# Query-key scores: casting loads of four heads replaced by float32 loads of eight heads that GpSimd casts and interleaves

## The chip, the cores and the metric

The kernel runs on one core of one Trainium2 chip. The metric is the device time of the kernel in microseconds (us), as the median of several runs. Engine names are those of the profile: PE is TensorE, PEld its weight loads, DVE is VectorE, ACT is ScalarE, POOL is GpSimd, SP is SyncE. "L106" is line 106 of the kernel that was profiled.

## The reference

```python
# q and k: (8, 12, 1024, 64) float32, normal random numbers times 0.1
def reference(q, k):
    return np.einsum('bhid,bhjd->bhij', q, k).astype(np.float32)
```

There are 96 heads. Each needs a 1024x1024 float32 score matrix from two 1024x64 inputs. The kernel reads 50.33 MB and must write 402.65 MB, so it is mostly a kernel that writes.

## The kernel before

Heads are taken in batches of four (the first three batches have 1, 1 and 2 heads). The loads are issued by GpSimd, and they cast: they read float32 from memory and leave float16 in the core's own memory. PE transposes q in pairs of 64 columns, and k twice, so that every transposed k row exists in both halves of the 128 rows. Score matmuls then alternate between the two halves. DVE copies the transposes out of PSUM, ACT and DVE copy the scores, and SP issues one 4 MB output transfer a head.

```python
    in_pool = ctx.enter_context(tc.tile_pool(name="in_pool", bufs=4))
    out_pool = ctx.enter_context(tc.tile_pool(name="out_pool", bufs=4))
    ...
        def load(self):                                   # class Batch
            rows = slice(self.first * S, (self.first + self.G) * S)
            self.q_sb = in_pool.tile([P, GMAX * NT, D], F16, tag="q")
            self.k_sb = in_pool.tile([P, GMAX * NT, D], F16, tag="k")
            for src, dst in ((qf, self.q_sb), (kf, self.k_sb)):
                nc.gpsimd.dma_start(
                    out=dst[:, : self.R],
                    in_=src[rows].rearrange("(p r) d -> p r d", p=P),
                )
        def transpose(self, a):
            ...
            for e in range(4):
                r = a * NT + 2 * e
                nc.tensor.transpose(t_ps[:, e], self.q_sb[:, r : r + 2], ident)
            for t in range(NT):
                rows = self.k_sb[:, a * NT + t]
                nc.tensor.transpose(t_ps[0:64, 4 + t], rows, ident)
                nc.tensor.transpose(t_ps[64:128, 4 + t], rows, ident)
            ...                                           # DVE: G copies to qT, one to kT
        def scores(self, g):
            o_sb = out_pool.tile([P, NT, S], F32, tag="out")
            for t in range(NT):
                h = (t % 2) * 64                          # alternating half of the rows
                ps = po_pool.tile([P, S], F32, tag="po")
                for n in range(2):
                    nc.tensor.matmul(ps[:, n * 512 : (n + 1) * 512],
                                     qT[h : h + 64, g, t // 2],
                                     kT[h : h + 64, g, n * 512 : (n + 1) * 512])
                ...                                       # t in (1, 4, 6): DVE copies, else ACT
            nc.sync.dma_start(out=..., in_=...)           # 4 MB, one head
    ...
    AHEAD = 3                                             # loads three batches ahead
```

The output pool holds four buffers of 32 KB for each partition. That is the queue of work that keeps the DMA engines busy when something else stalls.

## Time and profile before

| | before |
|---|---|
| time, median of 3 runs | 1070.94 us (1070.71 to 1071.27) |
| DMA busy share | 9 tenths or more in all 40 slices but the last |
| loading queue's share of 16 engines | 11.9% |
| output: issue to landing | 36.7 us |
| PE / DVE / ACT / POOL busy | 59 / 53 / 44 / 3% |

These are lines of the profile's page: busy time by engine, then the rows of 40 equal slices of the span (a digit is the busy share in tenths), the DMA queues, the summary of the chain of waits, three groups of instructions (busy us, mean ns of one, idle time before them and what ended most of it), and the output's DMA issues.

```profile
PE 627.9 (59%) x3456; PEld 214.0 (20%) x3456; DVE 565.7 (53%) x758; ACT 468.4 (44%) x481; POOL 28.2 (3%) x58
...
DMA  9999999999999999999999999999999999999996
GB/s 213 394 382 386 380 400 414 394 420 396 410 410 384 422 398 410 411 389 419 401 397 424 390 419 401 400 419 389 415 406 399 422 430 430 429 434 432 431 431 292
...
q1 hardware_dynamic: 13824, 402.66, 88.0%
q0 software_dynamic: 7488, 25.17, 11.9%
q8 instruction: 27, 0.44, 0.1%
...
DMA 77%; PE 7%; ACT 7%; DVE 1%; issue 0%; ACTq 0%
...
L106 PE MATMUL ps<-kT,qT 64*128 64x512 f16 x1536 | 480.9, 597 | 270.8 <-ACT o_sb L114 227.2
...
L91 DVE COPY qT<-t_ps 128x128 f16<-128x128 f16 (+1 forms) x374 | 121.2, 469 | 95.7 <-PE t_ps L82 95.7
L92 DVE COPY kT<-t_ps 128x1024 f16<-128x1024 f16 x96 | 118.8, 1237 | 0.0
...
out_dram<-o_sb SPq DMA_DIRECT2D x96, 4096.0 KB, 36.7
```

The DMA engines are the bottleneck: no other engine is above 59%, and the DMA row has no hole. (The rate reads 380 to 420 GB/s while loads run, because the casting loads count with the 25.17 MB that they write, not the 50.33 MB that they read; after the last load it is about 431.) The Trainium skill, "DMA: Bandwidth & Descriptors", section "Where 436 GB/s comes from", puts the ceiling of the fabric at 435 GB/s, and the trace agrees: the slices without loads, but for the last, reach 429 to 434.

The chain of waits (start, duration, what) shows the same thing in time. One long output transfer follows another with about 6 us of PE and ACT between them, in which the other queued outputs keep the engines busy.

```profile
793.69 38.04 DMA out_dram<-o_sb
...
835.00 1.48 PE ps L106 x4
...
837.53 34.88 DMA out_dram<-o_sb
```

Three windows of before: the columns are the window, its length, busy time of PE, PEld, DVE, ACT and POOL with counts, the granted PE clock, the DMA share and GB/s. The first is in the middle, and the other two are at the end, where the engines finish one after another.

```profile
322.00:330.00 8.00, 5.22 (x36) 2.06 (x33) 5.27 (x8) 4.17 (x5) 0.56 (x2) 0.50 1.01 400
...
1062.00:1066.00 4.00, 0.00 (x0) 0.00 (x0) 0.00 (x0) 0.00 (x0) 0.00 (x0) 0.50 0.19 82
1066.00:1070.00 4.00, 0.00 (x0) 0.00 (x0) 0.00 (x0) 0.00 (x0) 0.00 (x0) 0.50 0.02 8
```

### The profile page before, as it was taken

To read this page: it belongs to the slowest core of one execution; us is meant where nothing else is said; L and a number is where in the kernel's file an instruction comes from. 1 tells how busy PE (TensorE), PEld (TensorE's weight loads), DVE (VectorE), ACT (ScalarE), POOL (GpSimd) and SP (SyncE) were. 2 spreads that over 40 slices of the span, in tenths; PEclk is the share of its full clock that TensorE was granted. 3 is DMA by queue.
4 is the path that set the end of the run, shared out by engine and by line. 5 is a ranking of instruction groups with operands and counts; after the bars stand their busy time and mean duration, and the time that the engine had idled before them with its cause. 6 is when DMAs were issued, how large, how long until landed. Compare 5 with 4: busy or idle time off the path is not lost.

```text
span 1069.6 us, 8844 instructions
## 1 busy us (share of the span) xinstructions
PE 627.9 (59%) x3456; PEld 214.0 (20%) x3456; DVE 565.7 (53%) x758; ACT 468.4 (44%) x481; POOL 28.2 (3%) x58
## 2 busy tenths in 40 slices
PE   6786455565654656557465564655656567667530
PEld 2222121121211212212122121221211212212100
DVE  5676445464653646547455464554655646655420
ACT  4454344444533445344443444444444445454530
POOL 3000000000000000000000000000000000000000
PEclk8565555555555555555555555555555555555555
DMA  9999999999999999999999999999999999999996
GB/s 213 394 382 386 380 400 414 394 420 396 410 410 384 422 398 410 411 389 419 401 397 424 390 419 401 400 419 389 415 406 399 422 430 430 429 434 432 431 431 292
DMA packets 21353, 428.39 MB, mean 401 GB/s; under 512 B 2368, under 2 KB 2880, under 8 KB 9024
## 3 DMA queue, kind: packets, MB, share of 16 engines
q1 hardware_dynamic: 13824, 402.66, 88.0%
q0 software_dynamic: 7488, 25.17, 11.9%
q8 instruction: 27, 0.44, 0.1%
q14 instruction: 14, 0.11, 0.0%
HBM read 50.33 MB, written 402.65 MB: 424 GB/s over the span
## 4 chain that ended last, share of the span: by engine, by line
DMA 77%; PE 7%; ACT 7%; DVE 1%; issue 0%; ACTq 0%
DMA out_dram<-o_sb 77%; ACT o_sb L114 7%; PE ps L106 6%; DVE kT L92 0%; DVE qT L91 0%; PE t_ps L81 0%; PE t_ps L78 0%; DVE o_sb L112 0%; PE t_ps L82 0%; ACTq L114 0%
## 5 line engine op out<-in xcount | busy, mean ns | idle before, releaser
L114 ACT COPY o_sb<-ps 128x1024 f32<-128x1024 f32 x480 | 467.1, 1014 | 566.5 <-DMA out_dram<-o_sb 359.1
L106 PE MATMUL ps<-kT,qT 64*128 64x512 f16 x1536 | 480.9, 597 | 270.8 <-ACT o_sb L114 227.2
L112 DVE COPY o_sb<-ps 128x1024 f32<-128x1024 f32 x288 | 351.7, 1223 | 374.0 <-DMA out_dram<-o_sb 213.8
L106 PEld LDWEIGHTS <-qT 64*128 64x128 f16 x1536 | 101.0, 109 | 605.2 <-issue 580.0
L91 DVE COPY qT<-t_ps 128x128 f16<-128x128 f16 (+1 forms) x374 | 121.2, 469 | 95.7 <-PE t_ps L82 95.7
L78 PE MATMUL t_ps<-ident,q_sb 128*128 128x128 f16 x384 | 56.4, 299 | 135.9 <-DVE kT L92 130.2
L92 DVE COPY kT<-t_ps 128x1024 f16<-128x1024 f16 x96 | 118.8, 1237 | 0.0
L81 PE MATMUL t_ps<-ident,k_sb 128*64 128x128 f16 x768 | 102.5, 310 | 0.0
L82 PE MATMUL t_ps<-ident,k_sb 128*64 128x128 f16 x768 | 102.4, 310 | 0.0
L81 PEld LDWEIGHTS <-k_sb 128*64 128x64 f16 x768 | 77.5, 165 | 19.8 <-issue 19.4
L82 PEld LDWEIGHTS <-k_sb 128*64 128x64 f16 x768 | 77.4, 164 | 7.5 <-issue 7.5
L78 PEld LDWEIGHTS <-q_sb 128*128 128x128 f16 x384 | 34.6, 127 | 187.2 <-issue 121.3
L64 POOL DMA_DIRECT2D q_sb<-in_q_dram x26 | 14.0, 537 | 767.5 <-PE t_ps L78 766.8
L64 POOL DMA_DIRECT2D k_sb<-in_k_dram x26 | 13.9, 534 | 13.2 <-PE t_ps L82 13.2
L114 ACT ACT_TABLE_LOAD x1 | 1.3, 1283 | 0.7 <-PEq L157 0.7
masks.py:199 POOL TENSOR_SCALAR_AFFINE_SELECT ident<-ident 128x128 f16<-128x128 f16 x1 | 0.4, 362 | 0.0
masks.py:197 POOL MEMSET ident<- 128x128 f16 x1 | 0.3, 271 | 0.0
L157 POOL MEMSET const-float32-0.0<- 128x1 f32 x1 | 0.1, 98 | 0.2 <-issue 0.2
L157 POOL MEMSET const-bfloat16-1.0<- 128x1 bf16 x1 | 0.1, 101 | 0.0
L157 POOL MEMSET const-uint8-127<- 128x1 uint8 x1 | 0.1, 101 | 0.0
L157 POOL MEMSET const-float32-1.0<- 128x1 f32 x1 | 0.1, 98 | 0.0
## 6 DMA issues: line engine op xcount, KB each, us to landing
out_dram<-o_sb SPq DMA_DIRECT2D x96, 4096.0 KB, 36.7
q_sb<-in_q_dram POOLq DMA_DIRECT2D x23, 512.0 KB, 18.1
k_sb<-in_k_dram POOLq DMA_DIRECT2D x23, 512.0 KB, 29.4
q_sb<-in_q_dram POOLq DMA_DIRECT2D x2, 128.0 KB, 3.5
k_sb<-in_k_dram POOLq DMA_DIRECT2D x2, 128.0 KB, 3.6
q_sb<-in_q_dram POOLq DMA_DIRECT2D x1, 256.0 KB, 6.3
k_sb<-in_k_dram POOLq DMA_DIRECT2D x1, 256.0 KB, 7.0
```

The costliest lines, as they stand in the source:

```text
L64: nc.gpsimd.dma_start(out=dst[:, : self.R], in_=src[rows].rearrange("(p r) d -> p r d", p=P),)
L78: nc.tensor.transpose(t_ps[:, e], self.q_sb[:, r : r + 2], ident)
L81: nc.tensor.transpose(t_ps[0:64, 4 + t], rows, ident)
L82: nc.tensor.transpose(t_ps[64:128, 4 + t], rows, ident)
L91: nc.vector.tensor_copy(out=qT[:, g, :, :, a], in_=t_ps[:, 0:4, ms])
L92: nc.vector.tensor_copy(out=kT[:, :, :, a], in_=t_ps[:, 4:12].rearrange("c t (g m) -> c g m t", g=G),)
L106: nc.tensor.matmul(ps[:, n * 512 : (n + 1) * 512], qT[h : h + 64, g, t // 2], kT[h : h + 64, g, n * 512 : (n + 1) * 512],)
L112: nc.vector.tensor_copy(out=o_sb[:, t], in_=ps)
L114: nc.scalar.copy(out=o_sb[:, t], in_=ps)
L157: nc = _bacc.Bacc("TRN2", target_bir_lowering=False, num_devices=1)
```

## The change

The intent: plain float32 loads instead of casting ones, issued by ACT and SP instead of GpSimd; the idle GpSimd does the cast. Heads come in blocks of eight, in two halves of four. The cast writes head a of the first half beside head a of the second half, so that one 128x128 transpose serves two heads and k need not be transposed twice. A block has four loads of 8 KB a partition (q and k of each half), but only three raw buffers fit, so the fourth load of a block waits for the first cast of that block. There is only one float16 block buffer.

```diff
-    in_pool = ctx.enter_context(tc.tile_pool(name="in_pool", bufs=4))
+    in_pool = ctx.enter_context(tc.tile_pool(name="in_pool", bufs=3))
+    half_pool = ctx.enter_context(tc.tile_pool(name="half_pool", bufs=1))
 ...
+        def load(self, n, eng, raw=None):
+            if raw is None:
+                x_sb = in_pool.tile([P, self.elems], F32, tag="x")
+                raw = x_sb
+            self.raw[n] = raw
+            start = (self.first + n // 2 * self.G) * S
+            src = (qf, kf)[n % 2][start : start + self.G * S]
+            eng.dma_start(out=raw, in_=src.rearrange("(p r) d -> p (r d)", p=P))
 ...
+        def cast(self, n):
+            nc.gpsimd.tensor_copy(
+                out=self.halves[n % 2][:, :, n // 2],
+                in_=self.raw[n].rearrange("p (r d) -> p r d", d=D),
+            )
 ...
-            for e in range(4):
-                r = a * NT + 2 * e
-                nc.tensor.transpose(t_ps[:, e], self.q_sb[:, r : r + 2], ident)
-            for t in range(NT):
-                rows = self.k_sb[:, a * NT + t]
-                nc.tensor.transpose(t_ps[0:64, 4 + t], rows, ident)
-                nc.tensor.transpose(t_ps[64:128, 4 + t], rows, ident)
+            for x, src in enumerate(self.halves):
+                for t in range(NT):
+                    nc.tensor.transpose(t_ps[:, x * NT + t], src[:, a * NT + t], ident)
 ...                                  (DVE: one copy of 128x1024 to qT, one to kT)
-                h = (t % 2) * 64
+            cs = slice(half * D, (half + 1) * D)          (all matmuls of a head in one half)
 ...
+    def refill(i):                                        (i: the block after the next)
+        if b:
+            half_sb = half_pool.tile([P, 2 * half_elems], F16, tag="half")
+            b.place(half_sb, 0)
+            for n in range(3):
+                b.cast(n)
+        yield                                             (one head later)
+        if b:
+            b.load(3, nc.scalar)
+            b.cast(3)
+        if c:                                             (c: the block after b)
+            c.load(0, nc.scalar)
+            c.load(1, nc.scalar)
+        yield
+        yield
+        if c:
+            c.load(2, nc.scalar)
```

The first eight heads are loaded in smaller pieces into a borrowed output buffer.

More of the change, by code (lines that the diff above doesn't have):

```diff
@@ L28 @@
     GMAX = 4
-    assert D == 64 and NT == 8 and BH % GMAX == 0
+    assert D == 64 and NT == 8 and BH % (2 * GMAX) == 0
     qf = q.rearrange("b h s d -> (b h s) d")
@@ L37 @@
     of = out.rearrange("b h i j -> (b h) i j")
-    sizes = [1, 1, 2] + [GMAX] * (BH // GMAX - 1)
-    assert sum(sizes) == BH
+    sizes = [1, 1, 2] + [GMAX] * (BH // (2 * GMAX) - 1)
+    assert 2 * sum(sizes) == BH
     consts = ctx.enter_context(tc.tile_pool(name="consts", bufs=1))
     ident = consts.tile([P, P], F16)
-    in_pool = ctx.enter_context(tc.tile_pool(name="in_pool", bufs=4))
+    in_pool = ctx.enter_context(tc.tile_pool(name="in_pool", bufs=3))
+    half_pool = ctx.enter_context(tc.tile_pool(name="half_pool", bufs=1))
     tr_pool = ctx.enter_context(tc.tile_pool(name="tr_pool", bufs=2))
@@ L53, with place @@
     )
-    class Batch:
+    class Block:
         def __init__(self, first, G):
             self.first, self.G, self.R = first, G, 8 * G
-        def load(self):
-            rows = slice(self.first * S, (self.first + self.G) * S)
-            self.q_sb = in_pool.tile([P, GMAX * NT, D], F16, tag="q")
-            self.k_sb = in_pool.tile([P, GMAX * NT, D], F16, tag="k")
-            for src, dst in ((qf, self.q_sb), (kf, self.k_sb)):
-                nc.gpsimd.dma_start(
-                    out=dst[:, : self.R],
-                    in_=src[rows].rearrange("(p r) d -> p r d", p=P),
-                )
+            self.elems = self.R * D
+            self.raw = [None] * 4
+        def load(self, n, eng, raw=None):
[6 more added lines that the diff above has]
+            eng.dma_start(out=raw, in_=src.rearrange("(p r) d -> p (r d)", p=P))
+        def place(self, half_sb, at):
+            n = 2 * self.elems
+            self.halves = [
+                half_sb[:, x * half_sb.shape[1] // 2 + at :][:, :n].rearrange(
+                    "p (r h d) -> p r h d", h=2, d=D
+                )
+                for x in range(2)
+            ]
+        def cast(self, n):
[3 more added lines that the diff above has]
+            )
         def alloc(self):
-            self.qT = tr_pool.tile([P, GMAX * 4 * P], F16, tag="qT")
+            self.qT = tr_pool.tile([P, GMAX * S], F16, tag="qT")
             self.kT = tr_pool.tile([P, GMAX * S], F16, tag="kT")
@@ L74, in transpose, with scores @@
             G, pp = self.G, P // self.G
-            t_ps = pt_pool.tile([P, 12, P], F16, tag="pt")
-            for e in range(4):
-                r = a * NT + 2 * e
-                nc.tensor.transpose(t_ps[:, e], self.q_sb[:, r : r + 2], ident)
-            for t in range(NT):
-                rows = self.k_sb[:, a * NT + t]
-                nc.tensor.transpose(t_ps[0:64, 4 + t], rows, ident)
-                nc.tensor.transpose(t_ps[64:128, 4 + t], rows, ident)
-            qT = self.qT[:, : G * 4 * P].rearrange(
-                "c (g e m a) -> c g e m a", g=G, e=4, m=pp
+            t_ps = pt_pool.tile([P, 2 * NT, P], F16, tag="pt")
+            for x, src in enumerate(self.halves):
+                for t in range(NT):
+                    nc.tensor.transpose(t_ps[:, x * NT + t], src[:, a * NT + t], ident)
+            qT = self.qT[:, : G * S].rearrange(
+                "c (g t m a) -> c g t m a", g=G, t=NT, a=G
             )
             kT = self.kT[:, : G * S].rearrange(
-                "c (g m a t) -> c g m a t", g=G, m=pp, t=NT
+                "c (g m a t) -> c g m a t", g=G, a=G, t=NT
             )
-            for g in range(G):
-                ms = slice(g * pp, (g + 1) * pp)
-                nc.vector.tensor_copy(out=qT[:, g, :, :, a], in_=t_ps[:, 0:4, ms])
+            nc.vector.tensor_copy(
+                out=qT[:, :, :, :, a],
+                in_=t_ps[:, :NT].rearrange("c t (g m) -> c g t m", g=G),
+            )
             nc.vector.tensor_copy(
                 out=kT[:, :, :, a],
-                in_=t_ps[:, 4:12].rearrange("c t (g m) -> c g m t", g=G),
+                in_=t_ps[:, NT:].rearrange("c t (g m) -> c g m t", g=G),
             )
-        def scores(self, g):
-            bh = self.first + g
-            qT = self.qT.rearrange("c (g e m) -> c g e m", e=4, m=P)
+        def scores(self, n):
+            half, g = divmod(n, self.G)
+            cs = slice(half * D, (half + 1) * D)
+            qT = self.qT.rearrange("c (g t m) -> c g t m", t=NT, m=P)
             kT = self.kT.rearrange("c (g j) -> c g j", j=S)
@@ L102, in scores @@
             for t in range(NT):
-                h = (t % 2) * 64
                 ps = po_pool.tile([P, S], F32, tag="po")
-                for n in range(2):
-                    nc.tensor.matmul(
-                        ps[:, n * 512 : (n + 1) * 512],
-                        qT[h : h + 64, g, t // 2],
-                        kT[h : h + 64, g, n * 512 : (n + 1) * 512],
-                    )
+                for j in range(2):
+                    js = slice(j * 512, (j + 1) * 512)
+                    nc.tensor.matmul(ps[:, js], qT[cs, g, t], kT[cs, g, js])
                 if t in (1, 4, 6):
@@ L115, in scores @@
             nc.sync.dma_start(
-                out=of[bh].rearrange("(p t) j -> p (t j)", p=P),
+                out=of[self.first + n].rearrange("(p t) j -> p (t j)", p=P),
                 in_=o_sb.rearrange("p t j -> p (t j)"),
             )
-    batches, first = [], 0
+    blocks, first = [], 0
     for G in sizes:
-        batches.append(Batch(first, G))
-        first += G
-    AHEAD = 3
-    for b in batches[:AHEAD]:
-        b.load()
-    make_identity(nc, ident)
-    batches[0].alloc()
@@ L130 @@
-    for a in range(batches[0].G):
-        batches[0].transpose(a)
-    for i, b in enumerate(batches):
-        if i + AHEAD < len(batches):
-            batches[i + AHEAD].load()
-        nxt = batches[i + 1] if i + 1 < len(batches) else None
+        blocks.append(Block(first, G))
+        first += 2 * G
+    early = out_pool.tile([P, NT, S], F32, tag="out")
+    raw = early.rearrange("p t j -> p (t j)")
+    half_elems = 2 * GMAX * NT * D
+    half_sb = half_pool.tile([P, 2 * half_elems], F16, tag="half")
@@ new lines, with refill @@
+    at = 0
+    for b in blocks[:3]:
+        for n in range(4):
+            piece = raw[:, 2 * at + n * b.elems :][:, : b.elems]
+            b.load(n, (nc.sync, nc.scalar)[n % 2], piece)
+        b.place(half_sb, at)
+        at += 2 * b.elems
+    for n in range(3):
+        blocks[3].load(n, (nc.sync, nc.scalar)[n % 2])
+    make_identity(nc, ident)
+    for b in blocks[:3]:
+        for n in range(4):
+            b.cast(n)
+    def refill(i):
+        b = blocks[i] if i < len(blocks) else None
+        c = blocks[i + 1] if i + 1 < len(blocks) else None
+        if b:
+            half_sb = half_pool.tile([P, 2 * half_elems], F16, tag="half")
+            b.place(half_sb, 0)
+            for n in range(3):
+                b.cast(n)
+        yield
[6 more added lines that the diff above has]
+        yield
+        yield
+        if c:
+            c.load(2, nc.scalar)
@@ L136 @@
+    blocks[0].alloc()
+    blocks[0].transpose(0)
+    todo = []
+    for i, b in enumerate(blocks):
+        nxt = blocks[i + 1] if i + 1 < len(blocks) else None
         if nxt:
             nxt.alloc()
-        for g in range(b.G):
-            b.scores(g)
-            if nxt:
-                for a in range(g * nxt.G // b.G, (g + 1) * nxt.G // b.G):
-                    nxt.transpose(a)
+        done = 0
+        for n in range(2 * b.G):
+            b.scores(n)
+            for job in todo:
+                next(job, None)
+            if nxt and done < nxt.G:
+                nxt.transpose(done)
+                done += 1
+                if done == nxt.G and i > 0:
+                    todo.append(refill(i + 2))
+                    next(todo[-1])
+                    if n == 2 * b.G - 1:
+                        next(todo[-1])
```

## The prediction

> **What bounds it now.** The DMA engines. The 40-slice table has DMA at 9 (90% or more) in all slices but the last; the chain of waits is 77% output DMA. PE is busy 59%, DVE 53%, ACT 44%, POOL 3%. An output transfer takes 36.7 us from issue to landing (DMA issues), and a freed buffer is refilled in about 5.8 us, so three transfers are always queued. By the DMA-queue lines the 402.66 MB of output take 88.0% of 16 engines' span (941 us) and the casting loads 11.9% (127 us for 50.33 MB read). The rate is at its ceiling: slices without loads move 429 to 434 GB/s; the Trainium skill, "DMA: Bandwidth & Descriptors", section "Where 436 GB/s comes from", gives 435 GB/s, and the trace agrees.
>
> **What moves.**
> - Loads: the same 50.33 MB are read, now written as float32. By the trace's DMA records a loading packet now takes 322 ns (8 KB read, 4 KB written), a plain 8 KB packet (instruction fetch) about 307 ns, an output packet 1213 ns for 32 KB. At 303 to 310 ns, 6144 packets over 16 engines take 116 to 119 us (estimate): 8 to 11 us less. This is the whole gain on the bottleneck. Output packets average 1225 ns beside loads, 1217 after the last: if the casting loads cause that, up to 5 us more.
> - Issue by ACT instead of GpSimd: the same page ("Issuing engines are not separate DMA queues") says this saves issue time only. No gain.
> - PE: transposes fall from 1920 to 768. Score matmuls of a head now sit in one half of the rows, so pairs no longer overlap: 6.9 us a head at half clock (estimate). PE stays below 75% busy. Off the path.
> - DVE: 240 us of transpose copies become 96 of 1024 columns at about 1.24 us, 119 us. Off the path.
> - POOL: 48 casts of mostly 128x2048, 100 to 200 us in all (estimate), for 28 us of DMA issues. Off the path.
> - ACT: its queue now holds waits for GpSimd's casts. Stalls up to 10 us a block are covered: three queued outputs last some 29 us, and a head takes 7 to 9 us to make against 9.8 us to send.
>
> **Critical path.** Four heads now take 44.4 us, against 39.4 us after the last load (spacing of transfers in the chain of waits). I expect 44.0, with DMA at 9 throughout. At the start 7.3 MB of loads come first, some 17 us of DMA work; the first output, now issued at 17.0 us, should come at 17 to 20, so little DMA idles. Weakest place: 40 to 80 us, where block 3 needs its fourth load and cast before its transposes; PE may stand 10 us, the queue should just cover it. The tail (DMA falling off over the last 9 us, engines ending unevenly) stays or shortens a little.
>
> **Prediction:** 1060 us (1% less), 8 in 10 between 1052 and 1072. Faster by over 2%: 0.05; within 2%: 0.90; slower: 0.05.
>
> **Right if:** the loads' queue falls from 11.9% to about 11% of the engines; output stays at 941 us or falls to 935; no DMA slice but the last below 9; DVE below 45%; GpSimd above 10% without a costly wait; outputs land in 35 to 39 us.
>
> **Wrong if:** a DMA slice near the start or at a block boundary falls (ACT held by a load waiting on a cast, or PE by a cast): slower. If float32 loads disturb output packets (above 1230 ns), the gain vanishes. If the uneven end comes from the software queue, several us more are gained.

## The result, and the profile after

The changed kernel took 1084.95 us (median of 4 runs, 1084.18 to 1085.65) against 1071.11 us of before on the same chip. It is slower by 1.3%. A ratio in this document is the mean time of one kernel's fast runs over that of the other's of the same rounds, so it is not quite the ratio of the medians: here 1.0128, with a 95% interval of 1.0111 to 1.0146.

These lines of the page of after answer to those of before.

```profile
PE 754.7 (70%) x2304; PEld 287.6 (27%) x2304; DVE 509.6 (47%) x384; ACT 473.9 (44%) x481; POOL 91.6 (8%) x62
...
DMA  9989999999999999999999999999999999999998
GB/s 368 420 374 366 409 368 434 428 424 434 432 408 419 428 432 434 430 429 391 434 433 424 434 433 424 397 435 431 426 433 433 388 443 424 428 425 440 429 428 373
...
q1 hardware_dynamic: 14976, 406.85, 87.6%
q10 hardware_dynamic: 6912, 46.14, 11.1%
q8 instruction: 18, 0.29, 0.1%
...
PE 38%; DMA 37%; DVE 11%; issue 4%; POOL 4%; ACT 2%; POOLq 0%; ACTq 0%; SPq 0%; DVEq 0%
...
L125 PE MATMUL ps<-kT,qT 64*128 64x512 f16 x1536 | 664.8, 626 | 59.0 <-ACT o_sb L129 42.3
...
L106 DVE COPY qT<-t_ps 128x1024 f16<-128x1024 f16 x48 | 110.6, 2305 | 87.0 <-PE t_ps L98 87.0
...
out_dram<-o_sb SPq DMA_DIRECT2D x96, 4096.0 KB, 26.2
```

Three readings matter. The DMA row still shows nines nearly everywhere, but the rate row, which should now stand at about 430 throughout because nothing casts any more, has dips to 366, 368, 391, 397 and 388. The chain of waits, which was 77% DMA, is now shared between PE and DMA. And an output lands 26.2 us after its issue instead of 36.7: the queue of outputs ahead of it is shorter, so it covers less. The chain by itself proves little: that of fourth_ahead below, which is as fast as before, has DMA 38% and PE 34% too.

The waits of after (engine, what waited, what it waited for; total us, times, longest) name the place:

```profile
PE t_ps L98 <- POOL half_sb L84: 177.4, 20, 14.1
POOL half_sb L84 <- DMA x_sb<-in_k_dram: 133.2, 11, 14.2
```

PE waits for casts, and the cast waits for a load of k, 11 times: once for every block of eight heads. The chain of waits around one such block (start, duration, what):

```profile
295.24 1.84 PE t_ps L98 x16
...
297.19 1.90 POOL half_sb L84
...
299.11 17.79 DMA x_sb<-in_k_dram
...
316.95 1.90 POOL half_sb L84
...
318.90 1.04 PE t_ps L98 x8
319.94 5.24 PE ps L125 x12
```

The last transposes of a block free its only float16 buffer at 297.1. Only then can the first cast of the next block run, and only that cast frees the raw buffer for the fourth load. The load is issued at 299.11 and lands 17.8 us later; meanwhile the engines are full of outputs and other loads (a DMA share of 0.99 from 300 to 316 us). Its cast follows, and then the transposes. The timeline of PE in the same stretch, where the bracket gives the idle time before and what ended it, shows what PE does meanwhile: nothing for 14 us.

```profile
303.78 1.03 PE L125 MATMUL ps<-kT,qT 64*128 64x512 f16 x2
318.90 1.04 PE L98 MATMUL t_ps<-ident,half_sb 128*128 128x128 f16 x8 [14.09 <-POOL half_sb L84]
```

PE has score matmuls of the current block left, but the transposes of the next block stand ahead of them in its instruction order. So a late cast also holds heads whose data are ready.

The DMA engines feel this later. The table is worked out from the records of issue and of the packets; outputs are counted from 0. "Ended" is the end of an output's last 32 KB packet. The landing that the profile's page counts comes 0.3 to 4 us after that; by it, too, outputs 4, 7, 9 and 25 of after are issued when no other is in flight.

| output | issued | ended | others not ended at issue | previous one ended |
|---|---|---|---|---|
| after, 24 | 293.8 | 323.7 | 2 | 310.1 |
| after, 25 | 324.5 | 340.6 | 0 | 323.7, 0.9 us before the issue |
| after, 4 | 73.7 | 85.0 | 0 | 66.2, 7.5 us before the issue |
| after, 9 | 144.8 | 162.4 | 0 | 139.5, 5.4 us before the issue |
| before, 25 | 286.8 | 319.4 | 2 | 309.6, 22.8 us after the issue |

Outputs 24 and 25 are 30.7 us apart in after, as long as the queue lasts. In the windows (columns as above) of after, the start is worst; in the middle the engines carry almost only loads for a while, at a lower rate. (The clock column's 1.00 is no reading: the trace of after holds no clock event at all.)

```profile
68.00:76.00 8.00, 5.98 (x24) 2.32 (x25) 4.44 (x5) 2.75 (x3) 0.00 (x0) 1.00 0.66 268
...
322.00:330.00 8.00, 7.48 (x19) 2.49 (x18) 3.83 (x4) 5.46 (x6) 0.00 (x0) 1.00 0.98 338
330.00:346.00 16.00, 15.94 (x40) 5.42 (x39) 8.57 (x7) 11.62 (x13) 0.00 (x0) 1.00 1.01 435
```

In 322 to 330 the engines are "busy" for 98% of the time but move 338 GB/s, against 435 just after. (This view counts a packet where it starts. With packets spread over their time, the share is 0.92 and the rate 312.) In this window 262 packets of loads and 17 of outputs start, and those of the loads take 397 ns on average, against a median of 309 in the run. A dry queue is better seen in the rate than in the share.

### The profile page after: what moved, and what is told of

Its sections match the earlier page's. It is cut to its first block, busy times and chain, and to the rows that moved or that the text cites. A ratio compares the mean times of both kernels' runs of the same rounds, so it can differ in the third digit from the quotient of the medians.

```text
span 1083.2 us, 6240 instructions
## 1 busy us (share of the span) xinstructions
PE 754.7 (70%) x2304; PEld 287.6 (27%) x2304; DVE 509.6 (47%) x384; ACT 473.9 (44%) x481; POOL 91.6 (8%) x62
## 3 DMA queue, kind: packets, MB, share of 16 engines
q10 hardware_dynamic: 6912, 46.14, 11.1%
## 4 chain that ended last, share of the span: by engine, by line
PE 38%; DMA 37%; DVE 11%; issue 4%; POOL 4%; ACT 2%; POOLq 0%; ACTq 0%; SPq 0%; DVEq 0%
PE ps L125 30%; DMA out_dram<-o_sb 23%; DMA x_sb<-in_k_dram 14%; PE t_ps L98 8%; DVE qT L106 5%; POOL half_sb L84 4%; DVE o_sb L127 4%; DVE kT L110 3%; ACT o_sb L129 2%; DMA early<-in_q_dram 0%; POOLq L226 0%; ACTq L129 0%; SPq L72 0%; DVEq L127 0%; POOLq L84 0%
## 5 line engine op out<-in xcount | busy, mean ns | idle before, releaser
L129 ACT COPY o_sb<-ps 128x1024 f32<-128x1024 f32 x480 | 472.6, 1014 | 568.8 <-PE ps L125 424.3
L125 PE MATMUL ps<-kT,qT 64*128 64x512 f16 x1536 | 664.8, 626 | 59.0 <-ACT o_sb L129 42.3
L127 DVE COPY o_sb<-ps 128x1024 f32<-128x1024 f32 x288 | 352.4, 1223 | 452.5 <-PE ps L125 391.9
L125 PEld LDWEIGHTS <-qT 64*128 64x128 f16 x1536 | 210.4, 140 | 473.2 <-issue 462.1
L98 PE MATMUL t_ps<-ident,half_sb 128*128 128x128 f16 x768 | 95.5, 311 | 235.1 <-POOL half_sb L84 177.4
L98 PEld LDWEIGHTS <-half_sb 128*128 128x128 f16 x768 | 77.2, 143 | 287.0 <-POOL half_sb L84 191.7
L106 DVE COPY qT<-t_ps 128x1024 f16<-128x1024 f16 x48 | 110.6, 2305 | 87.0 <-PE t_ps L98 87.0
L84 POOL CAST half_sb<-x_sb 128x2048 f16<-128x2048 f32 x44 | 82.1, 1893 | 754.6 <-PE t_ps L98 621.4
L110 DVE COPY kT<-t_ps 128x1024 f16<-128x1024 f16 x48 | 59.2, 1234 | 0.0
L84 POOL CAST half_sb<-early 128x512 f16<-128x512 f32 (+1 forms) x12 | 8.8, 755 | 5.3 <-DMA early<-in_q_dram 5.1
## 6 DMA issues: line engine op xcount, KB each, us to landing
out_dram<-o_sb SPq DMA_DIRECT2D x96, 4096.0 KB, 26.2
```

What stands on the lines that cost most here:

```text
L84: nc.gpsimd.tensor_copy(out=self.halves[n % 2][:, :, n // 2], in_=self.raw[n].rearrange("p (r d) -> p r d", d=D),)
L98: nc.tensor.transpose(t_ps[:, x * NT + t], src[:, a * NT + t], ident)
L106: nc.vector.tensor_copy(out=qT[:, :, :, :, a], in_=t_ps[:, :NT].rearrange("c t (g m) -> c g t m", g=G),)
L110: nc.vector.tensor_copy(out=kT[:, :, :, a], in_=t_ps[:, NT:].rearrange("c t (g m) -> c g m t", g=G),)
L125: nc.tensor.matmul(ps[:, js], qT[cs, g, t], kT[cs, g, js])
L127: nc.vector.tensor_copy(out=o_sb[:, t], in_=ps)
```

## The experiments

Two theories stood against each other. **Theory A, dry stretches:** the fourth load's round trip empties the output queue once a block. **Theory B, the loads themselves:** plain float32 loads cost the DMA engines no less than casting ones, or more, so the expected saving is missing or turned into a loss. A third was that the longer score matmuls on PE bound the kernel. The experiments ran in four groups; each group shared a chip and its runs of before, whose medians were 1070.67, 1070.90, 1070.81 and 1070.73 us. All kernels had at least four timed runs. "Wrong" means that the result is known to be wrong, and only the time is used.

### other_data: the fourth cast no longer waits for the fourth load

On the changed kernel; wrong. The load is still issued and still moves its bytes.

```diff
-            b.cast(3)
+            b.cast(3, src=1)        # reads the raw buffer of the second load instead
```

> The changed kernel, but the fourth cast of a refilled block reads the second raw buffer instead of the fourth load's (wrong result on purpose); the fourth load is still issued, with the same bytes, and no cast waits for it. Theory 1 (the fourth load can only be issued after the block's first cast, so the transposes wait 12 to 18 us for it and the output queue runs dry): the PE waits on the casts of over 10 us vanish, outputs are issued before the previous one lands everywhere after the start, and the time falls from 1085 to 1062 to 1070 us. Theory 2 (score matmuls that no longer run in pairs make PE too slow): stays at 1080 to 1086. Theory 3 (float32 loads cost the DMA engines more than casting ones): stays at 1078 to 1086.

Measured: 1076.56 us (1075.90 to 1077.99), ratio 1.0056. That is 8.4 us less than after. The round trip costs that much, but 5.9 us over before remain, so theory A is right and isn't all.

### half_matmul and half_columns: half the score work on PE

On the changed kernel; wrong. In the first, one matmul of 512 columns instead of two, with the copies reading those 512 columns twice; in the second, two of 256 columns, so that the number of instructions stays.

```diff
-                for j in range(2):
+                for j in range(1):                       # half_matmul
-                    js = slice(j * 512, (j + 1) * 512)
+                    js = slice(j * 256, (j + 1) * 256)   # half_columns, with range(2)
-                    nc.vector.tensor_copy(out=o_sb[:, t], in_=ps)
+                    nc.vector.tensor_copy(out=twice(o_sb[:, t]), in_=doubled(ps))   # both; ACT's copy too
```

> The changed kernel with one 512-column matmul per row tile instead of two, copied out twice (wrong result on purpose): PE's score time is halved, 3.5 us a head in place of 7, ACT and DVE copies keep their size, loads and casts are untouched. Theory 2 (PE too slow): falls to 1062 to 1072 us. Theory 1 (wait for the fourth load): the dry stretches once a block stay, 1078 to 1085 us.

> As the run with one matmul per tile, but with two matmuls of 256 columns, so that the number of PE instructions is that of the changed kernel and only PE's streaming time is halved (wrong result on purpose). The run before lowered the fetches of instructions (16 KB packets) from 18 to 12 as well. If the shorter PE time gave its 9 us: again 1074 to 1078 us. If the six fewer fetches (5.6 us on one DMA engine) gave most of it: 1080 to 1084 us.

Measured: half_matmul 1076.20 us (1074.63 to 1077.08), ratio 1.0049; half_columns 1077.16 us (1076.11 to 1079.05), ratio 1.0059. So 8.8 and 7.8 us less than after. A faster PE helps about as much as an earlier cast, and it is the time of PE that helps, not the smaller number of instructions. Taken alone this could mean that PE binds. The next run and fourth_ahead say otherwise: the gains don't add, and with the full PE work the time falls to that of before.

### other_data_half: both together

The edits of other_data and half_columns; wrong.

> The changed kernel with both cures: no cast waits for the fourth load, and PE streams 256 columns a matmul (wrong result on purpose); loads, bytes and instruction counts stay. If the excess of the changed kernel is 9 us of float32 loads, less some 8 us of saved fetches, plus dry stretches of the output queue, then with no dry stretch it should take 1068 to 1073 us. If above 1075 us something else in the changed kernel costs time.

Measured: 1074.54 us (1071.85 to 1076.09), ratio 1.0037. Both together give 10.4 us, not 8.4 + 7.8 = 16.2. They cure the same stretches from two sides: the one shortens the wait, the other fills heads faster before and after it. The traces show it: the idle time of the DMA engines, averaged over the 16, from 20 us on and without the last 30 us, is 12.7 us in after, 5.1 in other_data, 8.5 in half_columns and 2.2 here (2.5 in fourth_ahead, 0.0 in before). About 3.7 us over before remain when the stretches are nearly gone.

### fourth_ahead: the fourth load gets its own buffer, a block ahead

On the changed kernel; correct results. Four full raw buffers do not fit, but a 4 KB float16 buffer does. So the fourth load is a casting one into a buffer of its own, issued by GpSimd a block earlier.

```diff
+    y_pool = ctx.enter_context(tc.tile_pool(name="y_pool", bufs=1))
 ...
+            if raw is None and n == 3:
+                raw = y_pool.tile([P, self.elems], F16, tag="y")
+                eng = nc.gpsimd
 ...
-            for n in range(3):
+            for n in range(4):
                 b.cast(n)
         yield
-        if b:
-            b.load(3, nc.scalar)
-            b.cast(3)
         if c:
+            c.load(3, nc.gpsimd)
             c.load(0, nc.scalar)
```

> The changed kernel, correct, with the fourth load of each block issued a block ahead, as a casting load by GpSimd into a 4 KB float16 buffer (a fourth 8 KB one does not fit). Theory 1 (late fourth load): the once-a-block dry stretch goes away, 1073 to 1078 us, like the run with other data. If the gain there came from something else: 1081 to 1086 us.

Measured: 1071.30 us (1070.78 to 1073.13), ratio 1.0003 (0.9990 to 1.0016). Its waits and its output issues, against those of after:

```profile
PE t_ps L102 <- POOL half_sb L88: 72.3, 13, 15.1
...
POOL half_sb L88 <- DMA x_sb<-in_k_dram: 1.1, 1, 1.1
```

```profile
out_dram<-o_sb SPq DMA_DIRECT2D x96, 4096.0 KB, 32.6
```

The cast's wait for the load falls from 133.2 to 1.1 us, PE's wait for casts from 177.4 to 72.3, and 13.7 us come back, with the same PE work as in after (754.1 us against 754.7). That shows theory A with a correct kernel, and that PE did not bind by itself. The run is not quite pure: a quarter of the loads cast again, which may account for some 2 us of the 13.7 (a quarter of the 9 us measured next; an estimate).

### before_f32_loads and f32_from_pool: the loads alone

On the kernel before; correct results. Its four-head batches and PE layout stay; only the loads become float32, and GpSimd casts. Both load two batches ahead into four raw buffers. In the first SP and ACT issue the loads, in the second GpSimd.

```diff
+    raw_pool = ctx.enter_context(tc.tile_pool(name="raw_pool", bufs=4))
+    in_pool = ctx.enter_context(tc.tile_pool(name="in_pool", bufs=2))
-                nc.gpsimd.dma_start(
-                    out=dst[:, : self.R],
+                raw = raw_pool.tile([P, GMAX * NT, D], F32, tag="x")
+                eng.dma_start(                           # sync / scalar, or gpsimd
+                    out=raw[:, : self.R],
+        def cast(self):
+            ...
+                nc.gpsimd.tensor_copy(out=dst[:, : self.R], in_=raw[:, : self.R])
```

> The load part alone: the kernel before with its PE and DVE work, but plain float32 loads issued by ACT into four 8 KB buffers two batches ahead and cast by GpSimd. The prediction's step (plain packets save 8 to 11 us of DMA time): 1058 to 1063 us. The rival (packet records of the casting loads overlap with others, so they occupied the engines no longer than plain ones): 1066 to 1072 us. Theory 3 (float32 loads cost more): over 1075 us.

> The same float32 loads and casts, issued by GpSimd instead of ACT. If the 9 us that float32 loads cost come from the bytes written to SBUF (8 KB a packet instead of 4): stays at 1078 to 1082 us. If they come from the issuing queue (ACT in place of GpSimd): falls to 1069 to 1073 us.

Measured: before_f32_loads 1079.79 us (1079.46 to 1080.05), ratio 1.0084; f32_from_pool 1079.04 us (1078.89 to 1081.03), ratio 1.0081. Float32 loads, with the casts that they need and nothing else changed, cost 9 us here instead of saving 8 to 11. Which engine issues them doesn't matter. That is what the Trainium skill says in "DMA: Bandwidth & Descriptors", section "Issuing engines are not separate DMA queues".

Where are the 9 us? There is no dip in the middle of before_f32_loads: apart from the first and the last slice its rate is 423 to 438 GB/s. Counting outputs and loads by the bytes that they move, before and before_f32_loads have moved the same amount, to 0.2 MB, at every time looked at from 500 us on: 448.6 and 448.5 MB at 1050 us. They part only in the last 20 us. These are windows of before_f32_loads, where nothing computes any more:

```profile
1066.00:1070.00 4.00, 0.00 (x0) 0.00 (x0) 0.00 (x0) 0.00 (x0) 0.00 (x0) 0.50 0.06 25
1070.00:1074.00 4.00, 0.00 (x0) 0.00 (x0) 0.00 (x0) 0.00 (x0) 0.00 (x0) 0.50 0.06 25
```

A share of 0.06 is one engine of 16: for the last 12 us or so a single DMA engine works off what it has left, at 25 GB/s, while 15 stand idle. In the same windows before is at 0.02 and then done. Added up in engine time averaged over 16, the idle time of the last 30 us is 8.0 us in before and 16.4 us in before_f32_loads: 8.4 of the 9 us. f32_from_pool ends in the same way (15.7 us), and its loads are counted in the software queue q0, as those of before are. So neither the issuing engine nor the kind of queue makes the difference.

It is tempting to add that plain loads delay that engine. The records say otherwise. Every output has sixteen landing marks, taken here as one for each engine. For the last output, the sixteenth mark comes 12.1 us after the fifteenth in before_f32_loads, 8.4 in f32_from_pool and 1.7 in before; but in before_few_loads (next), where almost nothing is loaded, it comes 12.3 us later. In before_f32_loads the gap grows over the whole run: 0.7 us at output 4, 3.2 at 25, 7.5 at 50, 9.1 at 75. So one engine falls behind whether or not there are plain loads; what keeps it with the next (1.7 us) are casting loads all through the run. How they do that is not shown.

### before_few_loads: what the casting loads cost

On the kernel before; wrong. From the fifth batch on, the data of the fourth are used again, so 46.1 of the 50.3 MB are not read.

```diff
-        if i + AHEAD < len(batches):
-            batches[i + AHEAD].load()
+        if i + AHEAD == 3:
+            batches[3].load()
+        elif i + AHEAD < len(batches):
+            batches[i + AHEAD].q_sb = batches[3].q_sb
+            batches[i + AHEAD].k_sb = batches[3].k_sb
```

> The kernel before with loads for the first 8 heads only; later batches reuse them (wrong result on purpose): 46.1 MB less to read. If the casting loads occupy the engines as long as their packet records say, 22 of 23 pairs at 5.2 us, 114 us are saved and the rate of the loads was 405 GB/s; if they cost what the spacing of the transfers says, 5.0 us a batch, 110 us; if they run at the full rate of 434 GB/s, 106 us. So 957, 961 or 965 us. From 961 up a plain load could save at most some 4 us in all.

Measured: 976.51 us (975.80 to 977.58), ratio 0.9118. The casting loads of 46.1 MB cost 94.2 us by this, the plain ones of before_f32_loads 103.3 us. This is below what was expected of either. The numbers are too low: without loads, the outputs of the first 100 us come too slowly to fill the engines, and the trace has 13.0 us of idle engine time in the first 120 us, against 2.8 in before and 4.1 in before_f32_loads. And its end is uneven: 14.3 us of idle in the last 30, against 8.0 and 16.4. Allowing for both, the loads cost some 111 and 110 us (an estimate from these figures). So the two kinds cost about the same engine time, and the 9 us between the kernels are the end.

### casting_blocks and casting_ahead: the rest of the change without float32 loads

On the changed kernel; correct results. The loads cast again, issued by GpSimd, into float16 buffers of 4 KB; blocks of eight, PE layout and GpSimd's interleaving copies stay. casting_blocks has four buffers; casting_ahead has seven, with seven loads at the start and four after each block's copies.

```diff
-    in_pool = ctx.enter_context(tc.tile_pool(name="in_pool", bufs=3))
+    in_pool = ctx.enter_context(tc.tile_pool(name="in_pool", bufs=4))      # 7 in casting_ahead
-                x_sb = in_pool.tile([P, self.elems], F32, tag="x")
+                x_sb = in_pool.tile([P, 4 * S // 2], F16, tag="x")
 ...
-            for n in range(3):
+            for n in range(4):
                 b.cast(n)
-        ...
+        if c:
+            for n in range(4):
+                c.load(n, nc.gpsimd)                     # casting_ahead: the next four of a list
```

> The changed kernel's blocks, transposes and score matmuls, but with the casting loads of the kernel before, into float16 buffers that GpSimd then interleaves; all four loads of a block are issued one block ahead. Float32 loads cost 9 us, the late fourth load some 8 us, and the fewer instructions should save 8 us on one DMA engine. If all three hold, it beats both: 1059 to 1066 us. If the fetches don't matter: 1068 to 1073 us. If the slower PE layout matters by itself: above 1073 us.

> The blocks with casting loads again, now with seven 4 KB buffers, so that seven loads are on their way at the start and four more follow each block's copies; the earlier version ran dry for some 8 us between 100 and 150 us because block 4's loads were late. Without that and with 18 fetches: 1060 to 1067 us, faster than the kernel before. If still over 1072 us, the concentration of transposes at the start of a block is itself too much for the output queue.

Measured: casting_blocks 1079.75 us (1078.73 to 1080.22), ratio 1.0082; casting_ahead 1071.89 us (1069.74 to 1074.61), ratio 1.0013 (0.9995 to 1.0031). At first, casting_blocks seemed to say that the layout costs 9 us. Its trace says otherwise: outputs 7 and 9 are issued 9.3 and 5.1 us after the last packet of the one before had ended, from 106 to 115 us and from 142 to 147 us, since the loads of the fifth block came late. It had a dry stretch of its own. Loading further ahead took it away and 7.9 us with it. So the block of eight, the new PE layout and GpSimd's copies are together worth nothing measurable, in either direction.

### more_fetches: does fetching instructions delay one engine? (inconclusive)

The single late engine asked for a cause. PE's instructions are themselves fetched by DMA, in packets of 16 KB that take 0.93 us each by the records (the q8 line: 27 in before, 18 in after; that is one for every 256 of the 6912 and 4608 matmuls and weight loads). If those weigh on one engine, every fetch delays the end. This first test put 2304 one-column copies on GpSimd into before_f32_loads; correct results.

```diff
+            for x in range(24 * self.G):
+                nc.gpsimd.tensor_copy(out=scrap[:, x : x + 1], in_=self.k_sb[:, 0, 0:1])
```

> The kernel before with float32 loads, whose trace ends with a single DMA engine running some 12 us longer than the other 15, plus 2304 one-column copies on idle GpSimd, about 9 more instruction fetches of 16 KB and 0.93 us each. Theory 4 (all instruction fetches run on one DMA engine, and that engine sets the end): the time grows by some 8 us, 1086 to 1090, and the single-engine tail grows with it. Rival (fetches are spread over the engines, the slow engine has another reason): 1079 to 1081 us.

Measured: 1087.48 us (1085.98 to 1087.90), ratio 1.0153; 7.7 us over before_f32_loads. It does not decide anything: GpSimd's instructions are fetched by another queue (q14, 15 fetches become 33), in packets of 8 KB and 0.31 us, the q8 count stayed at 27, and the copies delayed the start by some 4 us.

### k_doubled, k_doubled_start and pe_more: fewer and more PE instructions, with casting loads

On the kernel before; correct results. In the first two GpSimd writes k twice side by side, so that 8 transposes of 128 columns replace 16 of 64; k_doubled_start doubles only the first batch before the loop, so that the start is not delayed. pe_more adds twelve one-column transposes to every head.

```diff
+            for x in range(2):                                          # k_doubled
+                nc.gpsimd.tensor_copy(
+                    out=self.k2_sb[:, : self.R, x], in_=self.k_sb[:, : self.R])
-                nc.tensor.transpose(t_ps[0:64, 4 + t], rows, ident)
-                nc.tensor.transpose(t_ps[64:128, 4 + t], rows, ident)
+                nc.tensor.transpose(t_ps[:, 4 + t], rows, ident)
 ...
+            for x in range(12):                                         # pe_more
+                nc.tensor.transpose(t_ps[0:1, 0], self.q_sb[:, a * NT, x : x + 1], ident)
```

> The kernel before, correct, with GpSimd doubling k's rows first so that one 128-column transpose does what two of 64 columns did: 1536 PE instructions fewer, about 6 of the 27 fetches of 16 KB. PE, DVE and GpSimd stay off the path. Theory 4 (these fetches, 0.93 us each, all fall on one DMA engine, which ends last and sets the time): 1064 to 1067 us and a shorter single-engine tail. Rival (they don't set the end): 1069 to 1072 us.

> The kernel before, correct, with k doubled by GpSimd (6 fetches fewer), but with the early loads issued ahead of the doubling, which had delayed the start by 3 us. If the delay hid the gain: 1065 to 1069 us, faster than the kernel before by 2 to 5 us. If fetches don't matter where loads cast: 1070 to 1072 us.

> The kernel before with 2304 more PE instructions (12 one-column transposes a head, overwritten, 1.3 us a head on an engine that is idle 40% of the time): about 9 more fetches of 16 KB. Theory 4: 1077 to 1080 us, with a longer single-engine tail. Rival: 1070 to 1072 us.

Measured: k_doubled 1071.50 us (1069.48 to 1072.23), ratio 1.0005; k_doubled_start 1070.21 us (1069.33 to 1073.94, six runs), ratio 1.0001 (0.9985 to 1.0018); pe_more 1073.13 us (1073.06 to 1074.42), ratio 1.0026. The fetches moved as intended, to 21 with fewer transposes and to 36 in pe_more, but the time hardly followed: nothing for six fewer, 2.3 us for nine more. With casting loads the theory of the fetches misses.

### f32_fewer_pe and f32_more_pe: the same with float32 loads

On before_f32_loads. The first transposes neighbouring pairs of k, 8 instead of 16, which is wrong; the second adds twelve one-column transposes a head, as pe_more did, and is correct.

```diff
-                nc.tensor.transpose(t_ps[0:64, 4 + t], rows, ident)         # f32_fewer_pe
-                nc.tensor.transpose(t_ps[64:128, 4 + t], rows, ident)
+                r = a * NT + min(t, NT - 2)
+                nc.tensor.transpose(t_ps[:, 4 + t], self.k_sb[:, r : r + 2], ident)
 ...
+            for x in range(12):                                             # f32_more_pe
+                nc.tensor.transpose(t_ps[0:1, 0], self.q_sb[:, a * NT, x : x + 1], ident)
```

> The kernel before with float32 loads (1079.8 us, one DMA engine alone for the last 12 us), with 8 transposes of k a head instead of 16 (wrong result on purpose): 1536 PE instructions, about 6 fetches of 16 KB, fewer. Theory 4 (the PE's fetches fall on that one engine): 1073 to 1076 us, and its lonely stretch shrinks by some 5 us. Rival (they are spread, or don't matter): 1078 to 1081 us.

> The same kernel with 2304 more PE instructions, about 9 more fetches, PE still under 75% busy. Theory 4: 1086 to 1090 us with a longer lonely stretch. Rival: 1079 to 1082 us.

Measured: f32_fewer_pe 1076.39 us (1075.51 to 1079.74), ratio 1.0053; f32_more_pe 1085.72 us (1083.81 to 1086.21), ratio 1.0131. Here the time seems to follow. The last two columns are worked out from the traces: how long after the fifteenth landing mark of the last output the sixteenth comes, and the idle engine time in dry stretches (from 20 us on, without the last 30).

| float32 loads, four-head batches | fetches on q8 | their summed time | kernel | last engine alone | dry stretches |
|---|---|---|---|---|---|
| f32_fewer_pe | 21 | 19.7 us | 1076.4 us | 6.6 us | 0.4 us |
| before_f32_loads | 27 | 25.0 us | 1079.8 us | 12.1 us | 0.8 us |
| f32_more_pe | 36 | 33.6 us | 1085.7 us | 9.9 us | 5.6 us |

From the first to the second row 5.3 us of fetches add 3.4 us, and from the second to the third 8.6 us of fetches add 5.9. That looks like a rule, but the traces don't bear it out. The step to f32_more_pe is not at the end: its last engine is alone for a shorter time, and 4.8 of the 5.9 us are dry stretches (it also starts 2.7 us later). The step from f32_fewer_pe is at the end, but the runs of that kernel lie between 1075.5 and 1079.7 us.

The records don't name the engine of a packet, but the landing marks tell enough. In the last 23 outputs of before_f32_loads, which land after all loads have, the last engine is at least 8.7 us behind the next, so it is always the same one. Its marks follow each other in 9.66 to 9.99 us. A fetch of 0.93 us on that engine would show as a step of about 10.6 us, and there is none, although five fetches fall in that time. It is the same in f32_from_pool, f32_more_pe and before_few_loads (at most 10.10 us, five or six fetches). So there the last engine doesn't lose its time to fetches; it is a little slow on nearly every output (9.85 us on average, against 9.69 for the marks before it). For the time before the loads end, the marks don't settle it.

## Why the prediction was wrong

The prediction was 1060 us, within 1052 to 1072; the result is 1084.95. The kernel is inside "within 2%", which was given 0.90, but the sign is wrong. Two steps failed.

**"This is the whole gain on the bottleneck" (8 to 11 us less for the loads).** The packet durations were right and the conclusion was not. A plain packet of 8 KB takes 309 ns in after (the median), as predicted (303 to 310). But the 322 ns of a casting packet are not time that the engine spends on it alone: the records overlap, so their sum overstates what casting loads cost. Added up over the run, the records of before exceed the time in which its engines are busy by 11.4 us an engine, those of before_f32_loads by 4.5. These 6.9 us eat up most of the 8.2 us by which the plain packets are shorter in sum. The spacing of the outputs had said so already. Between the ends of outputs 15 and 71, before sends four heads in 44.0 us; after needs 44.3, dry stretches included. (After the last load, four heads take 38.7 to 39.1 us in before. The prediction's 44.4 and 39.4 came from the chain of waits; the difference is the same.) From 300 to 800 us before moves 214.5 MB and before_f32_loads 215.0, which is worth about 1 us. The fall of the queue's share from 11.9 to 11.1% was predicted as proof and proves nothing: part of the early loads is now counted in q1, and with them the loads take some 130 us of engine time in after against 127 before. Loads that run alone in a dry stretch have long packets too, so that their average is 338 ns. Beyond the missing gain, float32 loads alone cost 9 us (before_f32_loads, f32_from_pool), nearly all of it at the end, where one engine runs on alone for 12 us. The prediction had said that the uneven end "stays or shortens a little", and had named the opposite risk, that several us more might be gained if it came from the software queue.

**"PE may stand 10 us, the queue should just cover it."** The place, the mechanism and the symptom were named, and the size was wrong. The prediction took three queued outputs to last 29 us and the stall to be up to 10 us. The stall is 14 us, and it is added to the time that the heads before and after it need: outputs 24 and 25 are issued 30.7 us apart. At the start the queue held one output or none, and outputs 4, 5, 7 and 9 came 7.5, 0.7, 2.0 and 5.4 us after the last packet of the one before had ended. The wait recurs for every block and not only between 40 and 80 us. Of the 12.7 us of idle engine time in dry stretches, 6.8 come before 120 us and 5.9 after. Taking the wait away gave 8.4 us (other_data), 10.4 us (other_data_half) and, with a correct kernel, 13.7 us of which some 2 are due to casting again (fourth_ahead).

**The sum.** It can be taken from the traces, as engine time in us averaged over the 16 engines. Packets are all packet records added up; the overlap is what they count twice.

| profiled run | packets | idle, first 20 us | dry stretches | idle, last 30 us | overlap | span |
|---|---|---|---|---|---|---|
| before | 1070.4 | 2.8 | 0.0 | 8.0 | -11.4 | 1069.6 |
| before_f32_loads | 1062.2 | 3.4 | 0.8 | 16.4 | -4.5 | 1078.0 |
| after | 1070.2 | 1.9 | 12.7 | 3.3 | -4.6 | 1083.2 |

(The rows close to 0.3 us.) The predicted 8 us are there, in the packets of before_f32_loads, and are lost to the smaller overlap and the uneven end. In after the packets are longer again, because those of loads in dry stretches are long, and the dry stretches add 12.7 us; its end is even, since by then no engine is late (the sixteenth mark comes 0.2 us after the fifteenth). That dry stretches let a late engine catch up fits this and was not tested. They can't be all of it: other_data_half, with 2.2 us of them, has an end of 8.7 us. Its 18 fetches instead of 27 are one difference from before_f32_loads; that they matter is not shown.

Point by point, for the rest:

- "PE stays below 75% busy. Off the path." It is at 70%. A head's 16 matmuls take 6.9 us (664.8 us for 1536 is 433 ns each, against 313 before, where pairs overlapped); that was the estimate. PE isn't the bound by itself (fourth_ahead, casting_ahead), but it isn't off the path either: a slower head refills the queue more slowly, and half_columns gains 7.8 us.
- DVE was to fall to 119 us of transpose copies. It took 170 us (110.6 + 59.2): the copy to kT takes 1234 ns as predicted, that to qT 2305 ns. Both move 128x1024 elements, but in another order; the one to qT writes every fourth element (as the small copies of before did). Whether that is the reason was not tested. DVE is at 47%, not below 45. Nothing hangs on it.
- POOL was to be above 10%. It is at 8%; a cast of 128x2048 takes 1893 ns. The Trainium skill, "GPSIMD Engine Reference", section "Engine selection", calls operations of one input on GpSimd roughly line-rate, and 0.92 ns an element (1893 / 2048) agrees; DVE's copy out of PSUM (L127) takes 1223 ns for 1024 elements (1.19 ns each). But "without a costly wait" failed.
- "No gain" from the issue by ACT: right (f32_from_pool).
- The first output was to be issued at 17 to 20 us: it came at 20.2. "Outputs land in 35 to 39 us": 26.2. That was the sign, visible on the page, that the queue was not full.
- The first line under "Wrong if", "PE [held] by a cast: slower", is what happened. It was given 0.05 for a loss of over 2%, and the range, which ended at 1072, left it 1 us.

**What stays open.** Why one engine falls behind, and why it does so less with casting loads all through the run, but not with plain ones. PE's fetches don't explain it alone: with casting loads six fewer gave nothing and nine more 2.3 us (with the last engine 5.8 us behind the next in pe_more, against 1.7 in before), and with plain loads none of the last five fell on that engine. The Trainium skill, in "DMA: Bandwidth & Descriptors", section "Latency and other measured facts", notes that two of the engines are usually slower and guesses that this is specific to descriptors made in software. That guess doesn't explain the late engine here: the end is as uneven with plain loads of the hardware queues (before_f32_loads, 16.4 us of idle engine time, no software queue in its trace) as with those of the software queue (f32_from_pool, 15.7), and less so with casting loads of the software queue (before, 8.0). Whether the late engine is one of the two that the page means is not known, as the records name no engine.

No version beats the kernel before by a margin that the runs can tell: fourth_ahead, casting_ahead and k_doubled_start tie with it.

## What to carry to other kernels

When one load of a block has to wait for a buffer that the same block's work frees, count its whole round trip (free, load, cast, transposes, the next head) against what the output queue still holds at that moment, also at the start, where it holds almost nothing; and if four buffers don't fit, a smaller one for the odd load is enough. Price a change of the DMA work by the spacing of the transfers in the steady part, not by summed packet times, since packets overlap. And read the rate beside the busy share, and the last 20 us beside the middle: a share of 0.06 is one engine that everybody waits for. Before blaming a change for such an end, look for it in the other runs on hand: before_few_loads had it too, with almost no loads.

## What the Trainium skill lacked or had wrong

- "Runtime: NRT & Kernel Launch", "Instruction fetch mechanics", tells how instructions are fetched, but neither it nor "DMA: Bandwidth & Descriptors" has the time that a fetch takes on a DMA engine. Here PE's come in 16 KB packets of 0.93 us, 27 of them in before (25.0 us of one engine's time in all).
- "DMA: Bandwidth & Descriptors", "Latency and other measured facts": the slow engines are put down, as a guess, to descriptors made in software. Here one engine ran on alone for 12.1 us with plain loads of the hardware queues (16.4 us of idle engine time in the last 30 us); the end was as uneven with plain loads of the software queue (15.7), less so with its casting loads (8.0), and one engine ran on for 12.3 us with almost no loads at all.
- The same page: no comparison of a load that casts on the way with a plain one of the same bytes. Here 214.5 MB move between 300 and 800 us with the first and 215.0 with the second, while the whole kernels take 1070.7 and 1079.8 us. How far the spans of packets overlap is not given either: with casting loads their sum exceeds the engines' busy time by 11.4 us an engine, with plain ones by 4.5.
- "TensorE: Matmul & The Clock Gate", "Wait — 56ns, not 53.3ns?", gives 426.7 ns for 512 columns on the cold array. After's matmuls agree with that: most start 426 or 427 ns apart, while its profile shows a granted clock of 1.00 throughout and its trace holds no clock event. The page's warning under "Seeing it yourself", that clock events can't be fully trusted, fits; it might add these signs: a clock that never changes in the records, and runs of one kernel (before_f32_loads) that show 0.544, 1.0, 0.753 and 0.538 with times within 0.6 us.
- The pages speak of strides by cache lines, but no time was found for a DVE copy from PSUM that writes every fourth float16 element: 2305 ns here for 128x1024, against 1234 ns for the copy of the same size to kT.
